# Windowed attention on one core: from one to two rows per partition in every load and store

## The chip, the cores and the metric

The kernel runs on one core of one Trainium2 chip. The metric is the time of the device in microseconds (us). In one execution, the profiled one, a trace is taken; its span is about 2 us shorter than the time. All runs quoted here are of the same ("fast") state. Engines: PE is the matrix engine, PEld its weight loads, DVE the vector engine, ACT the scalar engine, POOL issues the loads and SP the stores. The transfers themselves run on the core's 16 DMA engines.

## The reference

Attention inside windows of 64 tokens, on four sequences of 4096 tokens with vectors of 1536 numbers, all in fp32:

```python
B, S, D, W = 4, 4096, 1536, 64
q_w = q.reshape(B, nw, W, D)          # k_w, v_w alike
logits = np.einsum('bnwd,bnud->bnwu', q_w, k_w) * D ** -0.5
attn = softmax(logits)                # over the last axis
out = np.einsum('bnwu,bnud->bnwd', attn, v_w)
```

Three inputs and the output are 16,384 rows of 6 KB each: 302 MB to read, 100.7 MB to write. No data is used twice, so every kernel moves these 402.65 MB.

## The kernel before

It works on blocks of 128 rows (two windows), one row per partition. POOL loads q, k and v and casts them to bf16 on the way; PE transposes q and k; PE computes the scores transposed (keys on partitions); ACT takes the exponential of the two 64x64 diagonal blocks; PE multiplies with v; DVE and ACT scale by the reciprocal of the row sum; SP stores.

```python
for blk in range(NBLK):                               # 128 blocks
    t0 = blk * P
    nc.gpsimd.dma_start(q_bf, qf[t0:t0 + P, :])       # 128 rows of 6 KB, fp32 -> bf16
    nc.gpsimd.dma_start(k_bf, kf[t0:t0 + P, :])
    nc.gpsimd.dma_start(v_bf, vf[t0:t0 + P, :])
    ...                                               # 24 transposes, 4 evictions (3 DVE, 1 ACT)
    for c in range(DC):                               # 12 matmuls, 128 columns
        nc.tensor.matmul(sT[:, 0:P], kT[:, c, :], qT[:, c, :], start=..., stop=...)
    ...                                               # 2 exponentials, row sum, reciprocal
    for j in range(N_OUT_CH):                         # 3 matmuls, 512 columns
        nc.tensor.matmul(po, pT, v_bf[:, j * CW:(j + 1) * CW], start=True, stop=True)
        ...                                           # eviction with the scale
    nc.sync.dma_start(of[t0:t0 + P, :], o_sb)
```

The softmax here doesn't subtract the row's maximum and nothing guards it: scores larger than these inputs give would overflow.

## Time and profile before

| | before |
|---|---|
| time, median of 5 runs | 973.09 us (973.01 to 973.58) |
| DMA engines busy | 90% or more in 39 of 40 slices |
| PE, DVE, ACT, POOL busy | 55%, 35%, 32%, 21% |
| HBM traffic over the span | 414 GB/s |

The profile page of the kernel before: busy time of each engine; then the DMA share in 40 equal slices of the span (9 is 90% or more), the packet count, each DMA queue with its packets, megabytes on the on-chip side and the time of its packets as a share of 16 engines' span, and the traffic on the HBM side.

```profile
PE 538.6 (55%) x5056; PEld 400.1 (41%) x5120; DVE 340.4 (35%) x769; ACT 314.0 (32%) x641; POOL 203.4 (21%) x390
...
DMA  9999999999999999999999999999999999999997
...
q0 software_dynamic: 55296, 151.02, 79.2%
q1 hardware_dynamic: 18432, 100.67, 26.2%
q8 instruction: 40, 0.66, 0.2%
...
HBM read 301.99 MB, written 100.66 MB: 414 GB/s over the span
```

No compute engine is busy much over half the time, and the DMA engines always are. Queue 0 carries the loads: 49,152 rows and 384 x 16 = 6,144 small packets that report completion. Queue 1 carries the stores. Queue 8 is no data of ours: its kind is "instruction". The shares sum to over 100% because a packet's record overlaps with that of the next: a record lasts 248 ns, but at the rate of the run a row costs an engine only 235 ns.

The waits view of the kernel before (engine, line, what it waited for: us in total, times, longest) says the same from the other side:

```profile
PE ps_tr_t L77 <- DMA k_bf<-in_k_dram: 211.3, 65, 5.3
PE ps_tr_t L77 <- DMA q_bf<-in_q_dram: 150.4, 96, 5.9
```

PE waits for loads to land.

### The profile page before, as it was taken

Reading aid. Unit: us, or ns where it says so; the run is one execution under the profiler, and the core shown is the slowest. Engines: PE = TensorE matmul, PEld = TensorE weight load, DVE = VectorE, ACT = ScalarE, POOL = GpSimd, SP = SyncE. Lnnn points to the kernel's source line nnn. Section 1 sums busy time; section 2 is a strip of 40 time slices with the busy share of each in tenths; the row PEclk is TensorE's granted clock in tenths of the full one; section 3 lists DMA queues with packets and bytes.
Section 4 is the critical chain, followed back from the end, with each engine's and each line's share of the span. In section 5 each row is a group of like instructions: output and inputs, shape, how many; then the busy total and the mean of one; then the engine's idle time right before and its main releaser. Section 6 shows DMA issues by size and latency. Waiting matters only on the chain. (4 is left out here: it accounts for less than half of the span.)

```text
span 971.7 us, 13136 instructions
## 1 busy us (share of the span) xinstructions
PE 538.6 (55%) x5056; PEld 400.1 (41%) x5120; DVE 340.4 (35%) x769; ACT 314.0 (32%) x641; POOL 203.4 (21%) x390
## 2 busy tenths in 40 slices
PE   5565655646556556565554645546456465554554
PEld 3444434434444344343433434434334343443343
DVE  2333433334334333342333433334333333343332
ACT  2233332333323233242323333233233232333333
POOL 3221222212222122121221221212122112222220
PEclk8667777677676776776877778787787777777877
DMA  9999999999999999999999999999999999999997
GB/s 190 261 257 274 255 263 266 256 271 258 260 270 254 269 261 257 275 252 266 261 257 274 258 260 268 252 272 259 259 272 255 266 264 254 274 255 263 267 253 237
DMA packets 73791, 252.53 MB, mean 260 GB/s; under 512 B 8192, under 2 KB 8192, under 8 KB 73728
## 3 DMA queue, kind: packets, MB, share of 16 engines
q0 software_dynamic: 55296, 151.02, 79.2%
q1 hardware_dynamic: 18432, 100.67, 26.2%
q8 instruction: 40, 0.66, 0.2%
q14 instruction: 23, 0.19, 0.0%
HBM read 301.99 MB, written 100.66 MB: 414 GB/s over the span
## 5 line engine op out<-in xcount | busy, mean ns | idle before, releaser
L77 PE MATMUL ps_tr_t<-ident,k_bf 128*128 128x128 bf16 x1536 | 171.4, 267 | 253.0 <-DMA k_bf<-in_k_dram 211.3
L77 PEld LDWEIGHTS <-k_bf 128*128 128x128 bf16 x1536 | 136.2, 123 | 309.9 <-DMA k_bf<-in_k_dram 226.3
L77 PE MATMUL ps_tr_t<-ident,q_bf 128*128 128x128 bf16 x1536 | 169.1, 252 | 153.2 <-DMA q_bf<-in_q_dram 150.4
L119 ACT ACTIVATE o_sb<-ps_o_t,recip 128x512 f32<-128x512 f32 x256 | 161.9, 683 | 278.0 <-PE ps_o_t L107 278.0
L77 PEld LDWEIGHTS <-q_bf 128*128 128x128 bf16 x1536 | 120.1, 114 | 195.4 <-DMA q_bf<-in_q_dram 179.4
L80 DVE COPY kT<-ps_tr_t 128x768 bf16<-128x768 bf16 x256 | 142.8, 558 | 72.3 <-PE ps_tr_t L77 66.5
L87 PE MATMUL sT<-qT,kT 128*128 128x128 bf16 x1536 | 164.4, 259 | 1.2 <-DVE kT L80 0.3
L80 DVE COPY qT<-ps_tr_t 128x768 bf16<-128x768 bf16 x128 | 71.4, 558 | 265.9 <-PE ps_tr_t L77 263.6
L97 ACT ACTIVATE pT<-sT 64x64 bf16<-64x64 f32 x128 | 27.8, 217 | 360.6 <-PE sT L87 360.6
L107 PE MATMUL ps_o_t<-v_bf,pT 128*128 128x512 bf16 x320 | 132.2, 479 | 13.9 <-issue 13.8
L87 PEld LDWEIGHTS <-kT 128*128 128x128 bf16 x1536 | 124.1, 119 | 18.4 <-DVE kT L80 18.4
L65 POOL DMA_DIRECT2D q_bf<-in_q_dram x128 | 67.8, 529 | 258.9 <-PE sT L100 169.2
L66 POOL DMA_DIRECT2D k_bf<-in_k_dram x128 | 67.7, 529 | 256.7 <-DMA v_bf<-in_v_dram 89.6
L67 POOL DMA_DIRECT2D v_bf<-in_v_dram x128 | 67.6, 528 | 226.2 <-DMA q_bf<-in_q_dram 107.5
L102 DVE RECIPROCAL recip<-sT 128x1 f32<-128x1 f32 x128 | 21.5, 168 | 258.1 <-PE sT L100 255.8
L82 ACT COPY qT<-ps_tr_t 128x768 bf16<-128x768 bf16 x128 | 102.2, 798 | 12.8 <-PE ps_tr_t L77 11.6
L111 DVE TENSOR_SCALAR o_sb<-ps_o_t,recip 128x512 f32<-128x512 f32 x128 | 96.0, 750 | 19.8 <-PE ps_o_t L107 14.3
L107 PEld LDWEIGHTS <-pT 128*128 128x128 bf16 x384 | 35.9, 118 | 26.4 <-issue 19.8
L100 PE MATMUL sT<-ones_bf,pT 128*128 128x1 bf16 x128 | 25.2, 197 | 6.7 <-ACT pT L98 0.5
L98 ACT ACTIVATE pT<-sT 64x64 bf16<-64x64 f32 x128 | 27.9, 218 | 1.5
L100 PEld LDWEIGHTS <-pT 128*128 128x128 bf16 x128 | 13.6, 106 | 15.8 <-ACT pT L98 14.5
L96 DVE MEMSET pT<- 128x64 uint32 x128 | 14.2, 112 | 9.5
(8 smaller groups left out, 2.2 us busy)
## 6 DMA issues: line engine op xcount, KB each, us to landing
out_dram<-o_sb SPq DMA_DIRECT2D x128, 768.0 KB, 7.8
q_bf<-in_q_dram POOLq DMA_DIRECT2D x128, 384.0 KB, 19.3
k_bf<-in_k_dram POOLq DMA_DIRECT2D x128, 384.0 KB, 19.0
v_bf<-in_v_dram POOLq DMA_DIRECT2D x128, 384.0 KB, 19.9
```

What stands on the lines that cost most here:

```text
L65: nc.gpsimd.dma_start(q_bf, qf[t0:t0 + P, :])
L66: nc.gpsimd.dma_start(k_bf, kf[t0:t0 + P, :])
L67: nc.gpsimd.dma_start(v_bf, vf[t0:t0 + P, :])
L77: nc.tensor.transpose(ps[:, j], raw[:, c * P:(c + 1) * P], ident)
L80: nc.vector.tensor_copy(dst_sl, ps)
L82: nc.scalar.copy(dst_sl, ps)
L87: nc.tensor.matmul(sT[:, 0:P], kT[:, c, :], qT[:, c, :], start=(c == 0), stop=(c == DC - 1),)
L98: nc.scalar.activation(pT[W:P, W:P], sT[W:P, W:P], AF.Exp, scale=scale)
L100: nc.tensor.matmul(sT[:, P:P + 1], pT, ones_bf, start=True, stop=True)
L107: nc.tensor.matmul(po, pT, v_bf[:, j * CW:(j + 1) * CW], start=True, stop=True)
L111: nc.vector.tensor_scalar(out=o_sb[:, j * CW:(j + 1) * CW], in0=po, scalar1=recip, scalar2=None, op0=mybir.AluOpType.mult,)
L119: nc.scalar.mul(o_sb[:, j * CW:(j + 1) * CW], po, recip)
```

## The change

The intent is longer transfers and longer runs of contiguous memory. A superblock of 256 rows is laid out with rows 2p and 2p + 1 in partition p, so each partition's share is 12 KB contiguous in HBM. The price is that a window's 64 tokens now lie in 32 partitions and two "slots" (even and odd rows), so the scores and the product with v have to be taken slot by slot. The transposed evictions are divided evenly over DVE and ACT, the zeros of pT are written once, and the last superblock is done as two blocks of 128 rows. Core of the diff:

```diff
-    NBLK = (B * S) // P
+    SB = 2 * P
+    NSB = (B * S) // SB
...
-        nc.gpsimd.dma_start(q_bf, qf[t0:t0 + P, :])
+            nc.gpsimd.dma_start(x, src[t0:t0 + SB, :].rearrange("(p j) d -> p j d", j=2))
...
-            nc.tensor.matmul(sT[:, 0:P], kT[:, c, :], qT[:, c, :], ...)      # 12 per 128 rows
+                nc.tensor.matmul(sT[:, 0:n * P], kT[:, c, j, :],             # 24 per 256 rows,
+                                 qT[:, c, 0:n, :], ...)                      # 256 columns
...
+        for i in range(n):  # queries of slot i
+            for ch in range(N_OUT_CH):
+                for j in range(n):                                           # 12 per 256 rows
+                    nc.tensor.matmul(po, lhs[j], v2[:, j, cs], start=(j == 0), stop=(j == n - 1))
...
-        nc.sync.dma_start(of[t0:t0 + P, :], o_sb)
+            nc.sync.dma_start(of[t0:t0 + SB, :].rearrange("(p j) d -> p j d", j=2), o2)
```

Buffers: four each of q, k, v and output (128 rows) before; three each (256 rows) after. The score tiles in PSUM go from two buffers to three.

## The prediction

> **What bounds the kernel now.** The DMA engines. The page's slice rows show the DMA share at 9 (90% or more) in 39 of 40 slices, while PE is busy 55% of the span, DVE 35%, ACT 32%, POOL 21%. The windows view gives a DMA share of 1.07 from 20 to 950 us. The page counts 302 MB read from HBM and 100.7 MB written, 414 GB/s over 971.7 us. In the waits view PE waits longest for the landing of k_bf and q_bf (211 and 150 us).
>
> **How far from the floor.** The DMA-queue lines count 55,296 and 18,432 packets: 65,536 rows of 6 KB on the HBM side (49,152 loads, 16,384 stores) and 8,192 tiny semaphore packets. From 100 to 900 us the packet records give 235 ns of one engine per row, semaphores included (a single packet takes 248 ns, partly overlapped with the next). The Trainium skill ("DMA: Bandwidth & Descriptors", section "Where 436 GB/s comes from") states a ceiling of 435 GB/s; at it a row costs 226 ns. So about 9 ns per row (4%, 37 us in all) is overhead per descriptor, semaphore or queue switch.
>
> **What the change does.**
> 1. Every load and store moves two rows per partition: 128 x 3072 elements, 12 KB contiguous in HBM. In the built program both access patterns are merged, so I expect one packet of 12 KB for two of 6 KB. If half of the 9 ns goes, a row costs 230.5 ns: 65,536 x 4.5 / 16 = 18 us less. This is on the critical path, and nearly the only thing that is. It is an estimate; loads alone already run nearer the ceiling (about 422 GB/s) than stretches mixed with stores (416).
> 2. PE gets more work: 24 score matmuls per 256 rows become 256 wide, output matmuls go from 6 to 12, row sums from 2 to 4. From the timeline (0.50 us for six transposes, 0.27 us for a 512-wide matmul) I estimate 7.9 us per 256 rows before and 11 to 12 after, against 14.7 us of DMA. Hidden.
> 3. ACT: 4 transposed evictions at 0.80, 3 output evictions at 0.65, 8 exponentials near 0.22: 6.9 us per 256 rows. DVE about 4.9 us. Hidden.
> 4. POOL issues half as many loads, each 1.5 MB, with three buffers; up to two superblocks (22 us of loads) stay queued while one is computed. Enough.
> 5. Start and end: first packet about 4 us in, unchanged. The last superblock is done as two 128-row blocks, so the tail (last load landing to the end, about 6 us now) stays within 2 us.
>
> **Predicted time: 956 us**, 8 in 10 between 946 and 968. Chances: faster by over 2% (below 953.6 us) 0.33; within 2% 0.64; slower 0.03.
>
> **What would show the steps right.** Data packets halve and their mean time nearly doubles to 470 to 490 ns; HBM traffic rises from 414 to about 422 GB/s; DMA stays at 9 in all slices; PE busy rises to 65 to 75%; POOL busy falls; PE still waits for loads.
>
> **What would make it wrong.** Packets stay at 6 KB (descriptors are split): 968 to 973 us. A longer packet loses less than half of the overhead, because most is per byte or lies in HBM: 962 to 968. Or the overhead lies mostly in switching between load and store queues, or long transfers remove the dips at store onset: 945 to 952. PE, in order, waits for v before it transposes the next q: if its backlog passed two superblocks, DMA gaps would show in the slices and cost time.

## The result, and the profile after

| | before | after |
|---|---|---|
| time, median | 973.41 us (13 runs, 973.01 to 973.85) | 960.28 us (7 runs, 959.34 to 961.87) |
| ratio after / before | | 0.9867 (95% interval 0.9857 to 0.9877) |

A ratio is the mean time of one kernel's fast runs over that of the other's of the same rounds, so it is not quite the ratio of the medians. The change makes the kernel 1.3% faster, inside the predicted range and short of 2%.

The same lines of the page of the changed kernel:

```profile
PE 642.7 (67%) x5560; PEld 452.0 (47%) x5624; DVE 297.1 (31%) x583; ACT 439.6 (46%) x957; POOL 103.7 (11%) x201
...
DMA  9999999999999999999999999999999999999996
...
q0 software_dynamic: 28080, 151.01, 76.5%
q1 hardware_dynamic: 9360, 100.67, 25.4%
q8 instruction: 44, 0.72, 0.3%
...
HBM read 301.99 MB, written 100.66 MB: 420 GB/s over the span
```

The same megabytes travel in half as many packets. PE has more work and POOL half as much, and the DMA engines are still the limit in every slice but the last. The waits view has PE wait for q as before:

```profile
PE ps_tr_t L111 <- DMA q<-in_q_dram: 190.3, 63, 8.4
```

The packet records of the two traces can be split further. From 100 to 900 us the HBM traffic was 418.8 GB/s before and 426.0 GB/s after. Dividing the 402.65 MB by these rates gives 961.4 and 945.2 us. The spans were 971.7 and 958.9 us. So the steady rate gained 16.2 us, and start and end together lost 10.3 us before but 13.7 us after. That gives back 3.4 us, and 12.8 us remain. The start is not where it lies: measured against the steady rate, the first 100 us lost 4.4 us before and 4.3 after, the last 50 us 5.9 and 9.2.

The windows view shows the end: busy us of each engine with its instruction count, granted PE clock, DMA share, and GB/s (on-chip side), in four-us windows that end with the span. Before:

```profile
959.70:963.70 4.00, 3.29 (x33) 2.75 (x34) 1.98 (x4) 1.97 (x5) 0.00 (x0) 0.77 0.75 223
963.70:967.70 4.00, 1.87 (x20) 0.96 (x17) 1.48 (x3) 2.11 (x5) 0.00 (x0) 1.00 0.56 230
967.70:971.70 4.00, 0.00 (x0) 0.00 (x0) 0.00 (x0) 0.00 (x0) 0.00 (x0) 0.59 0.48 197
```

After:

```profile
942.90:946.90 4.00, 0.90 (x17) 0.72 (x13) 0.56 (x1) 1.23 (x3) 0.00 (x0) 0.61 0.60 214
946.90:950.90 4.00, 2.85 (x21) 1.99 (x22) 2.14 (x4) 1.04 (x2) 0.00 (x0) 0.53 0.24 48
950.90:954.90 4.00, 1.56 (x14) 0.60 (x11) 0.92 (x2) 2.15 (x5) 0.00 (x0) 1.00 0.48 197
954.90:958.90 4.00, 0.00 (x0) 0.00 (x0) 0.00 (x0) 0.00 (x0) 0.00 (x0) 0.82 0.48 197
```

In the changed kernel the DMA share falls to 0.60 and then to 0.24 from 942.9 us on, although POOL had issued its last load by 928 us. With work queued, most DMA engines had nothing left to do. The completion records say why. Each load leaves 16 completion records; I take one to come from each of the 16 DMA engines. The lag between the first and the last of the 16 records, averaged over the loads that land in a stretch:

| lag of a load, us | 20 to 120 us | 430 to 530 us | last 50 us | the last load |
|---|---|---|---|---|
| before | 2.3 | 5.5 | 8.9 | 8.0 |
| after | 1.6 | 5.2 | 9.8 | 11.1 |

The 16 engines start together and drift apart over the whole run. In the middle this costs nothing visible (the changed kernel moves 425.8 to 426.2 GB/s in each 100 us from 100 to 900), since each engine has loads queued ahead. At the end the kernel waits for the slowest. For the last load of the changed kernel, 6 records came within 1.0 us of the first and 8 came over 10 us after it. So there were two questions: is it the packet length that gained, and what makes the engines drift apart?

### The profile page after: what moved, and what is told of

The parts are those of the page before. It is cut to its first block, busy times and chain, and to the rows that moved or that the text cites. A ratio compares the mean times of both kernels' runs of the same rounds, so it can differ in the third digit from the quotient of the medians.

```text
span 958.9 us, 13861 instructions
## 1 busy us (share of the span) xinstructions
PE 642.7 (67%) x5560; PEld 452.0 (47%) x5624; DVE 297.1 (31%) x583; ACT 439.6 (46%) x957; POOL 103.7 (11%) x201
## 5 line engine op out<-in xcount | busy, mean ns | idle before, releaser
L111 PE MATMUL ps_tr_t<-ident,q 128*128 128x128 bf16 x1536 | 147.5, 253 | 231.3 <-DMA q<-in_q_dram 190.3
L94 ACT ACTIVATE o<-ps_o_t,recip 128x512 f32<-128x512 f32 x192 | 131.9, 687 | 343.4 <-PE ps_o_t L145 341.8
L145 PE MATMUL ps_o_t<-v,pT 128*128 128x512 bf16 x693 | 242.7, 468 | 10.8 <-DMA v<-in_v_dram 6.6
L111 PEld LDWEIGHTS <-q 128*128 128x128 bf16 x1536 | 120.9, 116 | 273.0 <-DMA q<-in_q_dram 196.0
L118 PE MATMUL sT<-qT,kT 128*128 128x256 bf16 (+1 forms) x1536 | 189.3, 273 | 0.4 <-ACT kT L84 0.3
L91 DVE TENSOR_SCALAR o<-ps_o_t,recip 128x512 f32<-128x512 f32 x192 | 138.4, 748 | 65.8 <-PE ps_o_t L145 60.0
L111 PE MATMUL ps_tr_t<-ident,k 128*128 128x128 bf16 x1536 | 120.0, 221 | 44.8 <-ACT qT L84 28.8
L84 ACT COPY kT<-ps_tr_t 128x768 bf16<-128x768 bf16 x128 | 102.2, 798 | 83.5 <-PE ps_tr_t L111 83.5
L111 PEld LDWEIGHTS <-k 128*128 128x128 bf16 x1536 | 98.4, 99 | 66.4 <-issue 52.3
L125 ACT ACTIVATE pT<-sT 32x64 bf16<-32x64 f32 x504 | 108.0, 214 | 35.9 <-PE sT L118 24.6
```

The lines of the kernel that those rows point to most:

```text
L84: nc.scalar.copy(dst, ps)
L91: nc.vector.tensor_scalar(out=dst, in0=po, scalar1=r, scalar2=None, op0=mybir.AluOpType.mult)
L94: nc.scalar.mul(dst, po, r)
L111: nc.tensor.transpose(ps[:, jj], raw[:, j, c * P:(c + 1) * P], ident)
L118: nc.tensor.matmul(sT[:, 0:n * P], kT[:, c, j, :], qT[:, c, 0:n, :], start=(c == 0), stop=(c == DC - 1))
L125: nc.scalar.activation(pT[a:b, :, a:b], sT[a:b, 0:2 * P].rearrange("p (j q) -> p j q", j=2)[:, :, a:b], AF.Exp, scale=scale)
```

## The experiments

Twelve kernels ran. "Before" ran beside each, at medians of 973.2 to 973.6 us.

### Packet length: pad_both, pad_loads, pad_stores, split_both

Theory: the gain is the 12 KB packets. Rival: it is the number of transfers, or the new arrangement of the compute. Padding the tiles by 32 bytes per slot keeps the compute and the number of transfers, but the two rows of a partition are no longer contiguous on the chip and cannot become one packet:

```diff
-        x = pool.tile([P, 2, D], BF16, tag=tag, name=tag)
+        x = pool.tile([P, 2, D + 16], BF16, tag=tag, name=tag)
-            nc.gpsimd.dma_start(x, src[...])
+            nc.gpsimd.dma_start(x[:, :, 0:D], src[...])
...
-        o2 = o_pool.tile([P, 2, D], FP32, tag="o2", name="o2")
+        o2 = o_pool.tile([P, 2, D + 8], FP32, tag="o2", name="o2")   # and o2[:, :, 0:D] stored
```

> The changed kernel with 32 bytes of padding behind each 1536-element slot of the load and store tiles, so that the two rows of a partition can no longer be merged: same compute, same number of transfers, but 6 KB packets again. Theory (the 12 KB packets make the gain): data packets go back to 65,536, steady rate back to about 419 GB/s, time 972 to 977 us. Rival (the gain comes from fewer transfers and semaphores, or from the new arrangement of the compute): stays near 960 us.

> Padding on the load tiles only: 49,152 load packets of 6 KB, 8,064 + 256 store packets of 12 and 6 KB. If each packet costs the same overhead (about 7.8 ns of one engine per packet saved), three quarters of the gain goes: 969 to 973 us. If the gain lies in the stores or in the load-store switching, it stays at 960 to 964.

> Padding on the store tile only. Per-packet theory: a quarter of the gain goes, 963 to 965 us. If stores or switching matter most: 969 or more. The sum of the losses of pad_loads and pad_stores should be that of pad_both.

split_both has no padding and issues one transfer per slot (`for j in range(2): dma_start(x[:, j, :], s2[:, j, :])`, stores alike).

> No padding, but each 12 KB transfer issued as two, one per slot, each 128 rows of 6 KB: 6 KB packets and twice the transfers and semaphore packets, as many as the kernel before has. If semaphore packets (about 20 ns each in the records) cost full engine time, this is 4,160 x 20 / 16 = 5 us above pad_both; if they hide behind the data, within 2 us of pad_both. Rival (compute arrangement makes the gain): 960.

| kernel | time, us | ratio to before (95%) | over the changed kernel |
|---|---|---|---|
| changed | 960.28 | 0.9867 (0.9857 to 0.9877) | |
| pad_stores | 964.42 | 0.9909 (0.9893 to 0.9926) | 4.1 |
| pad_loads | 967.49 | 0.994 (0.9925 to 0.9955) | 7.2 |
| pad_both | 972.18 | 0.9989 (0.9974 to 1.0004) | 11.9 |
| split_both | 976.69 | 1.0033 (1.0018 to 1.0048) | 16.4 |

The page of pad_both shows the packets back at 6 KB:

```profile
q0 software_dynamic: 52272, 151.01, 78.9%
q1 hardware_dynamic: 17424, 100.67, 26.2%
```

The compute of the changed kernel with 6 KB packets takes as long as the kernel before. The losses of the loads and the stores alone, 7.2 and 4.1 us, add up to 11.3 of the 11.9 us. Per packet of which an engine is spared, that is 7.2 us x 16 / 24,192 = 4.8 ns for loads and 4.1 us x 16 / 8,064 = 8.1 ns for stores (estimates from differences of medians, good to 1 or 2 ns). Loads gained less per packet than the equal shares I had expected: pad_loads missed its 969 to 973 us from below.

The steady rates, which leave out start and end, say so more strongly: 423.1 GB/s in pad_loads and 422.8 in pad_stores against 426.0 in the changed kernel, or 6.5 and 7.0 us over the whole traffic. Half of the steady gain comes from the stores, which are a quarter of the packets. In the kernel before, the half-microseconds from 100 to 900 us in which only loads ran moved 422.5 GB/s, and those with 30 to 60% of stores 415.4. So a cost of switching between loads and stores, which longer packets also make rarer, may be a part of what I call overhead per packet; no run here separates the two.

split_both has twice as many transfers, with nearly as many packets of every kind as the kernel before, and costs 4.5 us on top. Its steady rate was 418.7 GB/s (pad_both 419.8), which accounts for 402.65 MB / 418.7 - 402.65 MB / 419.8 = 2.5 us; the other 2 us lie at its start and end. It is also 3.3 us slower than the kernel before, at the same steady rate, and loses this at the ends (13.7 us against 10.3). pad_both has the same compute and lost only 11.1 us there, so the arrangement alone does not explain the 3 us. The rival falls: the new arrangement gains nothing. Nor is the padding itself to blame for pad_both, for split_both has none.

### The floor: data movement alone (dma_1, dma_2, dma_4)

These kernels move the same bytes in the same order with 1, 2 or 4 rows per partition, with three buffers each, and do nothing else. Their outputs are wrong, which doesn't matter for the times. A store waits for its three loads through three tiny copies.

```python
q2 = load(qf, t0, "q2"); k2 = load(kf, t0, "k2"); v2 = load(vf, t0, "v2")    # N rows per partition
nc.vector.tensor_copy(o2[:, 0, 0:2], q2[:, 0, 0:2])                          # k2, v2 alike
nc.sync.dma_start(of[t0:t0 + SB, :].rearrange("(p j) d -> p j d", j=N), o2)
```

> Data movement of the changed kernel alone (12 KB packets, the same bytes; a store follows three tiny copies that wait for the loads; the output is wrong on purpose). If the changed kernel's steady 426 GB/s is the limit of the DMA engines and not of waits for compute, the steady rate is 426 again and the time about 402.6 MB / 426 GB/s = 945 us plus 4 us of start and 2 to 4 of end: 950 to 953. If compute waits cost something in the steady state, the rate is over 428. The lag between the first and the last of a load's 16 completion records, which grew from 1 to 11 us over the run in the changed kernel: stays under 3 us if it comes from the fetching of PE instructions, grows alike if the 16 engines are unequal by themselves.

> Data movement alone with one row per partition: 6 KB packets and the transfer count of the kernel before. Packet and semaphore theory: steady 419 GB/s, 16 us over dma_2: 966 to 969.

> Data movement alone with four rows per partition: 24 KB on the HBM side, half the transfers again. If a packet of any size costs the same overhead, the next halving saves half of what the first did, about 8 us: 942 to 945, steady 430 GB/s. If packets are split above some size: as dma_2.

| kernel | packet, HBM side | time, us | steady GB/s | one engine per 6 KB row | lag, last 50 us |
|---|---|---|---|---|---|
| dma_1 | 6 KB | 971.02 | 420.1 | 234.0 ns | 5.7 us |
| dma_2 | 12 KB | 952.54 | 427.6 | 229.9 ns | 3.2 us |
| dma_4 | 24 KB | 943.80 | 431.4 | 227.9 ns | 1.2 us |

The fifth column is 16 x 6,144 bytes over the rate. The three values lie on one line: 225.8 ns per row and 8.2 ns per packet (its share of the completion packets included), since 225.8 + 8.2 / 1, / 2 and / 4 gives 234.0, 229.9 and 227.9. The Trainium skill, "DMA: Bandwidth & Descriptors", section "Where 436 GB/s comes from", states a ceiling of 435.2 GB/s, which is 225.9 ns per row. These runs agree with the figure: what is left when the overhead per packet is taken off is that ceiling. They do not show its reason. The page derives it from the ports on the on-chip side, where the loads, narrowed to bf16, brought the traffic to only 267 GB/s in dma_2; it is the HBM side, with the wider data, that runs near the figure. The page of dma_4 shows that even these packets stay whole (12,288 load packets and 32 x 3 x 16 completions):

```profile
q0 software_dynamic: 13824, 151.00, 75.8%
q1 hardware_dynamic: 4608, 100.67, 25.2%
```

dma_1 missed its expectation of 966 to 969 us; dma_2 and dma_4 met theirs in time, though the rate of dma_2 lies between its two cases (426, or over 428) and its lag just over 3 us. Without compute, halving the packets takes off 971.02 - 952.54 = 18.5 us, near the prediction's 18; 16.8 us of that is the steady rate, the rest lies at the end. The kernel before stands 2.4 us above its own floor (dma_1), the changed kernel 7.7 us above its own (dma_2).

### What separates the changed kernel from its floor: dma_2_pe and dma_2_wide

In dma_2 the lag grows only to 3.2 us. Theory: the drift comes from the program's own traffic. Queue 8 fetched 44 packets of 16 KB in the changed kernel; 0.72 MB over its 11,250 PE instructions is 64 bytes for each. dma_2 has no PE instructions and no queue 8 (7 packets of 8 KB on another queue, 14, are its only fetches after the start). So dma_2_pe adds 88 idle transposes per 256 rows, to nearly the same count of PE instructions. Rival: any PE work that holds a load's buffer would do the same. So dma_2_wide gives PE about the same time with fewer instructions:

```diff
-    PE_PER_256 = 88                                                   # dma_2_pe
+    PE_PER_256 = 26                                                   # dma_2_wide
-            nc.tensor.transpose(ps[:, i % 6], v2[:, i % N, (i % DC) * P:(i % DC + 1) * P], ident)
+            nc.tensor.matmul(ps, v2[:, i % N, (i % DC) * P:(i % DC + 1) * P], v2[:, i % N, 0:512], ...)
...                                                                   # ps: 512 fp32 columns
```

> As dma_2, with 88 PE transposes per 256 rows that nobody waits for but the next load into their buffer: as many PE instructions, and so instruction-fetch packets (44 of 16 KB), as in the changed kernel. Fetch theory: the lag grows to about 10 us again and the time is 4 to 8 us over dma_2. Rival (the lag is the engines' own): lag and time as in dma_2, within 1.5 us.

> As dma_2_pe, but the PE works the same time per 256 rows with 26 matmuls of 512 columns instead of 88 transposes: 3,330 PE instructions instead of 11,266, so about 13 instruction-fetch packets instead of 44. Fetch theory: the lag grows to about 4 us and the time is 953.5 to 956, a third of the 7.4 us that dma_2_pe lost. Rival (dma_2_pe lost its time because a buffer is held while the PE reads it): 959 to 961 again.

The pages of dma_2_pe, then dma_2_wide:

```profile
PE 455.6 (48%) x5632; PEld 444.7 (46%) x5632; DVE 40.2 (4%) x196; POOL 102.1 (11%) x198
...
q8 instruction: 44, 0.72, 0.3%
```

```profile
PE 505.4 (53%) x1664; PEld 190.9 (20%) x1664; DVE 40.3 (4%) x196; POOL 102.1 (11%) x198
...
q8 instruction: 13, 0.21, 0.1%
```

PE works no less in dma_2_wide than in dma_2_pe; it fetches less. The copy that waits for the last load of v, in the timelines of dma_2, dma_2_wide and dma_2_pe (start, us, engine, line, operation):

```profile
944.65 0.17 DVE L76 CAST o<-v 128x2 f32<-128x2 bf16 x1 [3.47 <-DMA v<-in_v_dram]
```

```profile
946.01 0.17 DVE L76 CAST o<-v 128x2 f32<-128x2 bf16 x1 [3.46 <-DMA v<-in_v_dram]
```

```profile
950.56 0.17 DVE L76 CAST o<-v 128x2 f32<-128x2 bf16 x1 [3.47 <-DMA v<-in_v_dram]
```

The last stores in this table are from the packet records:

| | PE fetch packets | time, us | last v landed | last store landed | lag, last 50 us |
|---|---|---|---|---|---|
| dma_2 | 0 | 952.54 | 944.7 | 949.6 | 3.2 |
| dma_2_wide | 13 | 956.84 | 946.0 | 950.9 | 4.9 |
| dma_2_pe | 44 | 959.97 | 950.6 | 955.6 | 10.9 |
| changed kernel | 44 | 960.28 | | 957.2 | 9.8 |

The whole times mislead here: dma_2_wide missed its expectation of 953.5 to 956 us. Its PE is still at work after the last store, as its timeline shows, so that its span ends 4.5 us after the last store landed, where that of dma_2 ends 1.2 us after; about 3.3 us of its time are waited for by no data:

```profile
945.97 8.56 PE L71 MATMUL ps<-v 128*128 128x512 bf16 x26 [7.32 <-DMA v<-in_v_dram]
```

Read where the data lands: 44 fetches cost 5.9 us, 13 cost 1.4 us, and holding the buffers for at least as much PE time costs no more than that. The lag follows the fetches too, and so does the steady rate: 427.6 GB/s in dma_2, 427.1 in dma_2_wide, 426.1 in dma_2_pe and 426.0 in the changed kernel. The theory stands for these kernels. The whole time of dma_2_pe is within 0.4 us of the changed kernel's, but it too includes idle PE work after the last store. By the last stores the changed kernel is 7.6 us behind dma_2 (957.2 against 949.6), and dma_2_pe 6.0 us. So the fetching of PE's instructions can account for most of what separates the changed kernel from its floor; this agreement alone does not prove that it does.

What a single fetch does can be read in the completion records of dma_2_wide, whose fetches lie 63 to 74 us apart. Sort the 16 records of each load, and average them over the loads between two fetches. Before the first fetch the latest record comes 1.1 us after the first. After one, two, three, four, five and six fetches, exactly one, two, three, four, five and six records come over 1.5 us late:

| fetches so far | the six latest of 16 records, us after the first |
|---|---|
| 0 | 0.7, 0.8, 0.8, 0.9, 1.0, 1.1 |
| 1 | 0.7, 0.8, 0.8, 1.0, 1.1, 2.4 |
| 2 | 0.8, 0.8, 1.0, 1.1, 2.3, 2.5 |
| 4 | 0.7, 0.8, 2.4, 2.5, 2.6, 2.8 |
| 9 | 2.1, 2.3, 2.4, 2.6, 3.0, 4.1 |
| 12 | 2.1, 2.3, 3.7, 4.0, 4.0, 4.6 |

After the ninth to the twelfth fetch one, two, three and four records are over 3.4 us late: the second round has begun. So in this run each fetch sets one engine back by some 1.5 us, the next fetch another one, and after eight fetches it seems to be the first one's turn again (the records do not name the engines). Those that fell behind do not catch up. In dma_2_pe 44 fetches over eight engines would be 5.5 each, or 8.3 us (an estimate from these 1.5 us); over its last 50 us eight of the 16 records were 7.8 to 10.7 us late and the other eight at most 2.4. Why a fetch costs 1.5 us when its own record lasts 0.94 us stays open.

The same reading bears on the lag that dma_1 has without any PE instruction: one of the 16 records of its last load came 6.2 us after the first and the others within 2.1. The pages of dma_1, dma_2 and dma_4 list a second instruction queue, presumably for the other engines' instructions:

```profile
q14 instruction: 14, 0.11, 0.0%
```

```profile
q14 instruction: 7, 0.06, 0.0%
```

```profile
q14 instruction: 4, 0.03, 0.0%
```

The lag of dma_1's latest record behind the median stays nearly level between these packets and steps up right after four of the 14: from 1.9 to 2.5 us at 406 us, from 2.5 to 3.3 at 565, from 3.4 to 4.4 at 727 and from 4.7 to 5.5 at 887. No run took queue 14 away, so this cause is argued and not shown. It would also explain why the kernel before, with 40 fetches of its own, stands only 2.4 us above dma_1: the end of dma_1 already waits for one late engine.

### Fewer PE instructions in the real kernel, and longer packets: packed and quad

packed transposes two neighbouring bf16 elements at once as one fp32 word, so that 24 transposes do for 256 rows instead of 48; the scores then read every second element:

```diff
-                        nc.tensor.transpose(ps[:, jj], raw[:, j, c * P:(c + 1) * P], ident)
+                        nc.tensor.transpose(ps[:, jj], raw[:, j, :].bitcast(FP32)[:, c * P:(c + 1) * P], ident)
...
+                kc = kT[:, c // 2, j, :].bitcast(BF16).rearrange("p (t e) -> p t e", e=2)
+                qc = qT[:, c // 2, 0:n, :].bitcast(BF16).rearrange("p j (t e) -> p j t e", e=2)
+                nc.tensor.matmul(sT[:, 0:n * P], kc[:, :, c % 2], qc[:, :, :, c % 2], ...)
```

> The changed kernel with the transposes done on pairs: two neighbouring bf16 elements are viewed as one fp32 word, so 24 transposes per 256 rows instead of 48, each written as one instruction that loads its own weights; scores read the pairs with a step of two. The program has 5,362 PE instructions instead of 11,250. Fetch theory: about 21 fetch packets instead of 44, the lag halves to 5 to 6 us, time 955 to 958. Rival (fetches don't matter to the real kernel): 959 to 961. If the fp32 transposes take four times as long, PE nears 90% busy and DMA gaps may cost it all.

quad is packed with q and k loaded four rows per partition. Their order can be put right for nothing but a strided write in the eviction of the transposes; v and the output stay at two rows, because their order must match the partitions of pT:

```diff
+        q4 = load(qk_pool, qf, t0, "q4", 4, 4)     # 512 rows, "(p j) d -> p j d", j=4; k4 alike
...
+                        # row 4p + j is, in half h = p // 64, token P' = 2(p % 64) + j // 2 of slot j % 2
+                        d = dst[:, cs, :, j % 2, :].rearrange("p c h (t b) -> p c h t b", b=2)
+                        for h in range(2):
+                            evict_T(d[:, :, h, :, j // 2], ps[:, :, h * 64:(h + 1) * 64])
```

> packed, with q and k loaded four rows per partition (24 KB packets; the order of the rows is put right in the eviction of the transposes), v and the output staying at two, v with four buffers. Going from two to four rows gained 8.7 us for all traffic in the runs without compute; here half of the traffic goes, so 4 us: 951 to 954, under both kernels. If the deeper granularity (3 MB of reads per transfer) costs at the end or stalls the PE: 955 to 960.

| kernel | time, us | ratio to before (95%) | steady GB/s | lag, last 50 us |
|---|---|---|---|---|
| packed | 956.30 (955.73 to 956.76) | 0.9823 (0.9807 to 0.9839) | 426.4 | 7.4 us |
| quad | 953.33 (953.22 to 953.59) | 0.9795 (0.978 to 0.9809) | 427.8 | 7.8 us |

Both give the right result. From the page of packed:

```profile
PE 675.5 (71%) x4088; PEld 442.7 (46%) x4088; DVE 297.2 (31%) x583; ACT 357.6 (37%) x957; POOL 103.7 (11%) x201
...
q8 instruction: 32, 0.52, 0.2%
```

I had expected 21 fetches and a lag of 5 to 6 us; there are 32 fetches, because each fp32 transpose still runs as a weight load and a matmul. Yet PE's records fall from 11,184 to 8,176, and the time falls by 4.0 us, with the steady rate nearly unchanged: what it gains is at the end (span minus 402.65 MB over the steady rate: 10.7 us, against 13.7). packed also changes the evictions and PE's timing, so it supports the fetch theory in the real kernel without isolating it. quad gains 3.0 us more, where half of dma_4's gain of 8.7 us over dma_2 would have been 4.4. It beats both kernels: 20.1 us under the kernel before of its rounds, 2.05% by the ratio, though the interval still reaches below 2%.

### The split end: last_0

```diff
-    LAST = 1
+    LAST = 0
```

> The changed kernel with the last 256 rows done as one superblock like all others, not as two blocks of 128. If splitting the end shortens it as meant (a smaller last store, 1.8 instead of 3.7 us, and less work behind the last load), this is 2 to 5 us slower: 962 to 965 us. Rival (the lag of the DMA engines, some 10 us at the end, makes the loads of the last two blocks land together, so that splitting gains nothing, or costs by its extra transfers): 958 to 961 us.

961.24 us (959.35 to 961.7), ratio 0.987 (0.9854 to 0.9887): not distinguishable from the changed kernel. Doing the last 256 rows in two pieces buys no time that these runs can see. In last_0 the last load landed 4.0 us earlier (945.5 us against 949.5 in the packet records), but the last store, twice as large, landed 0.5 us later.

## Why the prediction was right, and where its sum was off

It said 956 us and the result was 960.28, inside 946 to 968.

1. **The bound.** Right: DMA stays at 9 in every slice but the last, and PE still waits for loads.
2. **Packets.** Right: they halve and stay whole; a 12 KB packet took 474 ns (loads) and 472 ns (stores) from 100 to 900 us, predicted 470 to 490. A row costs 230.8 ns of an engine, predicted 230.5. In steady state that is 16.2 us against the 18 of the prediction. "Half of the 9 ns" was a good guess because nearly all of the 9 ns goes with the number of packets (completions and switches between loads and stores included): dma_1 to dma_4 give 8.2 ns.
3. **PE, ACT, DVE.** Right: PE was 67% busy (predicted 65 to 75). From 100 to 900 us PE was busy 546 us, or 10.1 us per 256 rows where 11 to 12 were estimated, with a granted clock that rose from 0.75 to 0.89 (why, no run tested). All of it stays hidden behind 14.8 us of DMA.
4. **POOL and the queue.** Right: busy share 21% to 11%, no gaps in the middle.
5. **Start and end.** This term was mis-sized. The prediction counted the end as the time from the last load to the last store, and its "about 6 us" was low: in the packet records the last load landed 7.7 us before the end of the span before, and 9.4 us after. That is within the 2 us allowed, but it is not the whole end. Most DMA engines run dry before the last load has landed, because half of them are some 10 us behind the others. Start and end together cost 10.3 us before and 13.7 us after. The prediction had no such term, and of the steady gain of 16.2 us it took back 3.4. Half of the 3.4 us is the longer time after the last load (9.4 against 7.7 us). Why the rest grew is not shown: the kernel before drifts too (8.9 us over its last 50, against 9.8), and pad_both, with the fetches and the lag of the changed kernel (9.8 us), lost only 11.1 us at start and end, so the lag alone does not set the loss.

Its alternatives: neither splitting of packets nor a PE backlog appeared. "Most is per byte or lies in HBM" is refuted by the dma runs; it is the ends that brought the time near that branch's 962. Whether a part of the overhead lies in switching between loads and stores is open.

## What to carry to other kernels

When the DMA engines are the limit, lay data out so that each partition's share is contiguous on both sides: it is the packet's length that counts most (twice as many transfers with the same packets cost 4.5 us, packets of half the length 11.9), and the gain halves with each doubling until the ceiling is near. Compare with a kernel that only moves the data before looking for more. Check whether the 16 completions of a transfer drift apart over the run: long unrolled instruction streams are fetched by the same DMA engines, and a kernel ends with the slowest of them.

## What the Trainium skill lacked or had wrong

- No page has a figure for the cost of fetching instructions beside saturated DMA engines. "Runtime: NRT & Kernel Launch", section "Instruction fetch mechanics", describes the fetching in blocks of 16 KiB, as on queue 8 here, and calls the cost of crossing into the next block mostly hidden. Here it was not: 44 fetch packets of 16 KB (0.18% of the bytes) made the last load land 5.9 us later, with the lag between a load's 16 completions at 10.9 us; 13 made it 1.4 us later, each setting one of eight engines back by some 1.5 us.
- "DMA: Bandwidth & Descriptors", section "Bandwidth", advises transfers of 1 MiB or more. Here the size of a transfer was not what counted most: pad_both, with the transfer sizes of the changed kernel but 6 KB packets, ran at 419.8 GB/s steady, the changed kernel at 426.0, and dma_4, with packets of 24 KB and transfers twice as large again, reached 431.4.
- The same page, section "Why small descriptors are slow (HBM only)", gives about 3 cycles per packet (3.5 ns, an estimate with the 850 MHz that the page gives for the fabric), and presents it as a matter of small descriptors. The fit here is 8.2 ns per packet with completions included, and 6 KB packets still ran 2.6% below 24 KB ones (420.1 against 431.4 GB/s).
- The same page, section "Latency and other measured facts", says that two of the 16 DMA engines are usually slower. In dma_1 one completion of 16 came 6.2 us late at the end; in the changed kernel 8 came over 10 us late. In dma_2_wide, fetches set eight engines back in turn. These records do not name the engines.
- "HBM Reference", section "Specifications (TRN2)", gives about 425 GB/s for a core that streams alone. Mixed loads and stores with 24 KB packets held 431.4 GB/s here.
